# Multiply and GELU on one core: an early store of the first 4096 columns, between two loads on the same queue

## The chip, the cores and the metric

The kernel runs on one NeuronCore of a Trainium2 chip. The metric is the device time of one execution in microseconds; lower is better. Times are medians of several executions. The profile is of one execution, taken by the hardware profiler.

## What is computed

Two float32 arrays of 1024 x 4096 are multiplied element by element, and the product goes through the tanh form of GELU. The output has the same shape and type.

```python
def reference(x, y):          # both (1024, 4096) float32
    z = x * y
    return (0.5 * z * (1 + np.tanh(np.sqrt(2 / np.pi) * (z + 0.044715 * z ** 3)))).astype(np.float32)
```

Each array has 16.78 MB, so 33.55 MB are read and 16.78 MB are written.

## The kernel before

*Layout.* Each of the 128 partitions holds 8 rows of the array, which makes 32768 columns a partition. All of x stays in the on-chip buffer `xs` (128 x 32768), is multiplied there in place, goes through GELU in place, and is stored from there. The buffer `ys` holds half as much (16384 columns), so the second half of y overwrites the first.

*Stages.* The transfers are listed at the top of the file. x is loaded in two halves (x0 and x1, 8.39 MB each). y is loaded as a half (y0) and two quarters (y1 and y2, 4.19 MB each); y1 goes to the first half of `ys`, y2 to the second. The output is stored in two halves, store 0 and store 1. Compute works in steps of 4096 columns (`STEP`), eight in all: VectorE multiplies a step (line 87) once the loads it belongs to have landed, and counts `sem_mul` up by one; ScalarE then applies GELU to the step (line 94) and counts `sem_act` up by one. No step waits for a store.

*Order of the transfers.* There is no scheduler: all transfers are issued by SP, on one queue, in the order written in the code. x0 and y0 are hoisted ahead of the start-up barriers (`_hoist`). Behind these comes x1. Then each of y1 and y2 waits on `sem_mul`, since it overwrites what earlier multiplies read: y1 waits for two multiplies, y2 for four (line 77). Behind both loads SP waits for four activations and issues store 0, waits for eight and issues store 1 (lines 98 to 100), and last waits for the completion of both stores.

*What the steps touch.* `X_LOADS`, `Y_LOADS`, `STEP` and `STORES` (lines 13 to 17) define the pieces; `load_x` and `load_y` issue loads; each transfer has a semaphore of its own that reaches 16 when all of it has landed.

Of the kernel before, what the change touches and what calls it, by code (L numbers as in the profile page):

```python
# [1 line left out]

# [4 lines left out]


F32 = mybir.dt.float32
GELU = mybir.ActivationFunctionType.Gelu_apprx_tanh  # L10


X_LOADS = [(0, 16384), (16384, 32768)]

Y_LOADS = [(0, 16384, 0), (16384, 24576, 0), (24576, 32768, 8192)]
STEP = 4096
STORES = [(0, 16384), (16384, 32768)]
Y_RING = 16384


def _hoist(nc, issued):

    here = nc.cur_bb.bb.instructions
    first = nc.main_func.blocks[0].instructions
    for ins in issued:
        del here[next(k for k, i in enumerate(here) if i is ins or i.name == ins.name)]
    engine = issued[0].engine
    at = next(
        k
        for k, i in enumerate(first)  # L30
        if i.engine == engine and type(i).__name__ == "InstDrain"
    )
    first[at:at] = issued


@with_exitstack
def kernel(
    ctx: ExitStack,
    tc: tile.TileContext,
    x: bass.AP,  # L40
    y: bass.AP,
    out: bass.AP,
):
    nc = tc.nc
    P = nc.NUM_PARTITIONS

    x_r = x.flatten_outer_dims().rearrange("(p a) c -> p (a c)", p=P)
    y_r = y.flatten_outer_dims().rearrange("(p a) c -> p (a c)", p=P)
    out_r = out.flatten_outer_dims().rearrange("(p a) c -> p (a c)", p=P)
    total_f = x_r.shape[1]  # L50


    tc.close()
    tc.compile()  # L54

    xs = nc.alloc_sbuf_tensor("xs", [P, total_f], F32).ap()
    ys = nc.alloc_sbuf_tensor("ys", [P, Y_RING], F32).ap()
    sem_x = [nc.alloc_semaphore(f"sem_x{i}") for i in range(len(X_LOADS))]
    sem_y = [nc.alloc_semaphore(f"sem_y{i}") for i in range(len(Y_LOADS))]
    sem_o = [nc.alloc_semaphore(f"sem_o{i}") for i in range(len(STORES))]  # L60
    sem_mul = nc.alloc_semaphore("sem_mul")
    sem_act = nc.alloc_semaphore("sem_act")

    def load_x(i):
        a, b = X_LOADS[i]
        return nc.sync.dma_start(out=xs[:, a:b], in_=x_r[:, a:b]).then_inc(sem_x[i], 16)  # L66

    def load_y(i):
        a, b, r = Y_LOADS[i]
        return nc.sync.dma_start(  # L70
            out=ys[:, r : r + b - a], in_=y_r[:, a:b]
        ).then_inc(sem_y[i], 16)

    _hoist(nc, [load_x(0).ins, load_y(0).ins])
    load_x(1)
    for i in (1, 2):
        nc.sync.wait_ge(sem_mul, (Y_LOADS[i][1] - Y_LOADS[1][0]) // STEP)
        load_y(i)

    n = 0  # L80
    for i, (a, b, r) in enumerate(Y_LOADS):
        for j, (xa, xb) in enumerate(X_LOADS):
            if xa <= a < xb:
                nc.vector.wait_ge(sem_x[j], 16)
        nc.vector.wait_ge(sem_y[i], 16)  # L85
        for c in range(a, b, STEP):
            nc.vector.tensor_mul(  # L87
                out=xs[:, c : c + STEP],
                in0=xs[:, c : c + STEP],
                in1=ys[:, r + c - a : r + c - a + STEP],  # L90
            ).then_inc(sem_mul, 1)
            n += 1
            nc.scalar.wait_ge(sem_mul, n)
            nc.scalar.activation(  # L94
                out=xs[:, c : c + STEP], in_=xs[:, c : c + STEP], func=GELU
            ).then_inc(sem_act, 1)

    for i, (a, b) in enumerate(STORES):
        nc.sync.wait_ge(sem_act, b // STEP)
        nc.sync.dma_start(out=out_r[:, a:b], in_=xs[:, a:b]).then_inc(sem_o[i], 16)  # L100
    for i in range(len(STORES)):
        nc.sync.wait_ge(sem_o[i], 16)
    nums = sorted(s.num for s in [*sem_x, *sem_y, *sem_o, sem_mul, sem_act])
    assert nums == list(range(nums[0], nums[-1] + 1))
    nc.sync.sem_clear(range(nums[0], nums[-1] + 1))


# [1 line left out]
_INS = ['x', 'y']  # L109
_OUTS = [((1024, 4096), 'float32')]  # L110


# [23 lines left out]
```

## Time and profile before

| | us |
|---|---|
| median of 4 executions | 120.97 (120.87 to 121.22) |
| the profiled execution | 120.84 |
| its span, from the first instruction to the last | 119.5 |
| VectorE, mean of one multiply (x8) | 4.421 |
| ScalarE, mean of one activation (x8) | 3.617 |
| issue to landing: x0 and x1 | 21.9 and 58.7 |
| issue to landing: y0, y1, y2 | 40.8, 20.2, 22.0 |
| issue to landing: store 0 and store 1 | 37.7 and 26.1 |

The span lies within the profiled execution's time; what is outside it is start and end of the launch. Issue to landing runs from the issuing instruction on SP to the last of the 16 semaphore counts, so it holds the time that a transfer stood in the queue behind others. DMA share is the mean busy share of the 16 DMA engines of the core. In a cut of the span into stretches each packet counts where it begins, so a cut through a packet gives odd rates, and stretches are to be cut where the packets of a transfer begin.

### The profile page before, as it was taken

How to read it: one execution, taken by the hardware profiler on the slowest of the kernel's cores; microseconds unless marked ns; L12 is line 12 of the kernel's file. 1: busy time of each engine (PE TensorE's matmuls, PEld its weight loads, DVE VectorE, ACT ScalarE, POOL GpSimd, SP SyncE). 2: the span in 40 equal slices, each digit the busy share in tenths (PEclk: the TensorE clock that was granted, in tenths of full speed). 3: DMA queues.
4: the chain of work that ended last, by engine and by line, in shares of the span. 5: the costliest groups of instructions: out<-in, count | busy, mean ns of one | idle time of the engine just before them, and what ended most of it. 6: DMA issues, size and time to landing. Idle time of an engine off the chain costs nothing.

```text
span 119.5 us, 68 instructions
## 1 busy us (share of the span) xinstructions
DVE 35.0 (29%) x8; ACT 30.2 (25%) x9; POOL 0.2 (0%) x4
## 2 busy tenths in 40 slices
DVE  0000000000000199999600049949990000000000
ACT  3000000000000006797780000977479200000000
POOL 0000000000000000000000000000000000000000
DMA  9889888988899889988898989898899888988890
GB/s 351 351 351 702 351 351 351 680 373 351 351 570 483 351 351 504 548 351 351 373 504 351 526 351 515 362 526 351 351 504 548 351 351 373 680 351 351 351 680 22
DMA packets 1008, 50.33 MB, mean 421 GB/s; under 512 B 112, under 2 KB 112, under 8 KB 112
## 3 DMA queue, kind: packets, MB, share of 16 engines
q1 hardware_dynamic: 1008, 50.33, 98.5%
HBM read 33.55 MB, written 16.78 MB: 421 GB/s over the span
## 4 chain that ended last, share of the span: by engine, by line
DMA 53%; DVE 22%; ACT 3%; SPq 0%; issue 0%; DVEq 0%
DMA ys<-in_y_dram 53%; DVE xs L87 22%; ACT xs L94 3%; SPq L66 0%; DVEq L85 0%
## 5 line engine op out<-in xcount | busy, mean ns | idle before, releaser
L87 DVE TENSOR_TENSOR xs<-xs,ys 128x4096 f32<-128x4096 f32 x8 | 35.0, 4421 | 54.7 <-DMA ys<-in_y_dram 54.7
L94 ACT ACTIVATE xs<-xs 128x4096 f32<-128x4096 f32 x8 | 28.9, 3617 | 61.1 <-DVE xs L87 61.1
L94 ACT ACT_TABLE_LOAD x1 | 1.3, 1283 | 1.9 <-PEq L54 1.9
L120 POOL MEMSET const-bfloat16-1.0<- 128x1 bf16 x1 | 0.1, 101 | 0.0
L120 POOL MEMSET const-uint8-127<- 128x1 uint8 x1 | 0.1, 101 | 0.0
L120 POOL MEMSET const-float32-0.0<- 128x1 f32 x1 | 0.1, 98 | 0.2 <-issue 0.2
L120 POOL MEMSET const-float32-1.0<- 128x1 f32 x1 | 0.1, 98 | 0.0
## 6 DMA issues: line engine op xcount, KB each, us to landing
ys<-in_y_dram SPq DMA_DIRECT2D x2, 4096.0 KB, 21.1
xs<-in_x_dram SPq DMA_DIRECT2D x2, 40.3
out_dram<-xs SPq DMA_DIRECT2D x2, 31.9
ys<-in_y_dram SPq DMA_DIRECT2D x1, 40.8
```

The source lines that it names most:

```text
L87: nc.vector.tensor_mul(out=xs[:, c : c + STEP], in0=xs[:, c : c + STEP], in1=ys[:, r + c - a : r + c - a + STEP],).then_inc(sem_mul, 1)
L94: nc.scalar.activation(out=xs[:, c : c + STEP], in_=xs[:, c : c + STEP], func=GELU).then_inc(sem_act, 1)
L120: nc = _bacc.Bacc("TRN2", target_bir_lowering=False, num_devices=1)
```

## The change

The output is stored in three pieces instead of two: columns 0 to 4096, 4096 to 16384 and 16384 to 32768. The code that waits for the activations and issues a store becomes a function, `store(i)`. The first store is issued behind x1 and ahead of y1; the other two stay behind all loads. Loads and compute are as before.

```diff
-STORES = [(0, 16384), (16384, 32768)]
+STORES = [(0, 4096), (4096, 16384), (16384, 32768)]
...
+    def store(i):
+        a, b = STORES[i]
+        nc.sync.wait_ge(sem_act, b // STEP)
+        nc.sync.dma_start(out=out_r[:, a:b], in_=xs[:, a:b]).then_inc(sem_o[i], 16)
+
     _hoist(nc, [load_x(0).ins, load_y(0).ins])
     load_x(1)
+    store(0)
     for i in (1, 2):
         nc.sync.wait_ge(sem_mul, (Y_LOADS[i][1] - Y_LOADS[1][0]) // STEP)
         load_y(i)
...
-    for i, (a, b) in enumerate(STORES):
-        nc.sync.wait_ge(sem_act, b // STEP)
-        nc.sync.dma_start(out=out_r[:, a:b], in_=xs[:, a:b]).then_inc(sem_o[i], 16)
+    store(1)
+    store(2)
     for i in range(len(STORES)):
         nc.sync.wait_ge(sem_o[i], 16)
```

## The prediction

> **What bounds the kernel now.** I read the page first, then the chain of waits, the timeline with the landing times, and last the DMA share in stretches between the landings.
>
> The page says who is busy:
>
> ```profile
> DVE 35.0 (29%) x8; ACT 30.2 (25%) x9; POOL 0.2 (0%) x4
> DMA packets 1008, 50.33 MB, mean 421 GB/s; under 512 B 112, under 2 KB 112, under 8 KB 112
> q1 hardware_dynamic: 1008, 50.33, 98.5%
> ```
>
> The 16 DMA engines are occupied for 98.5% of the span and the compute engines for under a third. All bytes go over one queue, and the change moves the same 50.33 MB, so time can only come from how evenly that queue is fed and drained.
>
> The chain of waits names compute on the path (a share of 22% for VectorE), but that is the way the inference walks back: y loads wait for a multiply to free their buffer. The timeline shows that this wait is covered:
>
> ```profile
> 45.79 3.62 ACT L94 ACTIVATE xs<-xs 128x4096 f32<-128x4096 f32 x1 [42.58 <-DVE xs L87]
> 50.12 9.00 SPq L70 DMA_DIRECT2D ys<-in_y_dram  x2
> 62.44 31.20 SPq L100 DMA_DIRECT2D out_dram<-xs  x2
> 80.86 8.76 DVE L87 TENSOR_TENSOR xs<-xs,ys 128x4096 f32<-128x4096 f32 x2 [1.71 <-DMA ys<-in_y_dram]
> 89.66 3.62 ACT L94 ACTIVATE xs<-xs 128x4096 f32<-128x4096 f32 x1 [0.72 <-DVE xs L87]
> ```
>
> The reader should see that the second y load is issued at 50.12 and the first store at 62.44, each while earlier transfers still fill the queue. The groups by tile give issue-to-landing times, from which the landings follow: x0 at 21.9; y0 at 0.43 + 40.8 = 41.2; x1 at 1.93 + 58.7 = 60.6; y1 at 50.12 + 20.2 = 70.3; y2 at 58.79 + 22.0 = 80.8; store 0 at 62.44 + 37.7 = 100.1; store 1 at 93.30 + 26.1 = 119.4. The steps are 19.3, 19.4, 9.7, 10.5, 19.3, 19.3. One stands out: y2 carries the same 4.19 MB as y1 and takes 0.8 longer. It is the last load ahead of a store. Cut by where the packets of each transfer begin (x0, y0, x1, y1, y2, store 0, store 1; stretch, length, engines, clock, DMA share, GB/s):
>
> ```profile
> 1.00:21.00 20.00, 0.00 (x0) 1.28 (x1) 0.00 (x0) 1.00 1.01 419
> 21.00:40.30 19.30, 0.00 (x0) 0.00 (x0) 0.00 (x0) 1.00 1.00 435
> 40.30:59.70 19.40, 17.43 (x4) 11.75 (x4) 0.00 (x0) 1.00 1.00 432
> 59.70:69.40 9.70, 0.00 (x0) 2.72 (x1) 0.00 (x0) 1.00 1.00 432
> 69.40:79.80 10.40, 8.76 (x2) 4.23 (x2) 0.00 (x0) 1.00 1.00 403
> 79.80:99.10 19.30, 8.76 (x2) 10.24 (x3) 0.00 (x0) 1.00 1.00 435
> 99.10:118.40 19.30, 0.00 (x0) 0.00 (x0) 0.00 (x0) 1.00 1.00 435
> ```
>
> Loads and stores run at the same 432 to 435 GB/s. Only two stretches are below it: the first (20.0 instead of 19.3, the start of an empty queue) and y2's (10.4 instead of 9.7). In the second the share stays 1.00: no packet was missing, the last ones took longer. So the span is 1.0 before the first packet, 0.7 of start-up, 115.9 of bytes (5 x 19.3 for the large transfers, 2 x 9.7 for y1 and y2), 0.7 at the one turn from loading to storing, and 1.2 for the spread between the engines and the last completion.
>
> **What the Trainium skill says.** "DMA: Bandwidth & Descriptors", section Queues, rings and completion order: each DMA engine consumes its descriptors in ring order. The trace agrees: landings come in order of issue. So the new store will really stand between x1 and y1 and push y1 and y2 back. The section Two DMAs through the same engine are not ordered adds that descriptors are pipelined and an engine's read and write sides are separate queues; that fits the absence of any gap between y0 and x1 (435, then 432 GB/s)[...]. The section Latency and other measured facts gives about 0.6 us to a first byte for this kind of queue; here no packet begins before 1.0 us after the issue, and the trace's number is used.
>
> **The change part by part.** Numbering the stores anew: S0 (columns 0 to 4096, 2.10 MB), S1 (4096 to 16384, 6.29 MB), S2 (16384 to 32768, 8.39 MB).
>
> 1. *Instructions.* SP gets one more DMA and one more wait. The multiplies, the activations and every other DMA stay. On SP the new wait (first activation, done at 45.79 + 3.62 = 49.41) stands ahead of the y1 issue, which today goes at 50.12 when two multiplies are done. S0 costs SP about 0.35 (a store issue lasts 344 to 347 ns), so SP is free again at 49.8, before 50.12. No one waits longer. If it were later, the x1 load, which fills the queue until 59.7, would cover it by 9 us. Cost 0.
>
> 2. *Bytes.* S0 takes 2.10/435 = 4.8 us in the middle and the stores behind are shorter by the same 4.8. Net 0. The packets get smaller, 16 and 48 KB a row instead of 64 KB; from 64 to 32 KB the rate went from 435 (432 beside compute) to 432, so 0 to 0.1; I take 0.
>
> 3. *Turn from load to store.* It now happens twice, after x1 and after y2. The one seen cost 10.4 - 9.7 = 0.7. Add 0.7; bounds 0.5 to 0.8.
>
> 4. *Turn from store to load.* New, and not in the trace. Nearest row: the start of the queue, 20.0 - 19.3 = 0.7 for a first load whose reads have nothing in front of them. That is the upper bound (0.8 with rounding). The lower one is below nothing: if the 0.7 of step 3 only means that a store runs later in the pipeline than a load, the return gives it back (-0.7). I take +0.1: the y1 reads are queued 9 us before they are due, so an engine's read side can begin them while its write side still drains S0. If it then runs ahead of its writes by what the turn of step 3 cost (0.7), that hides all but 0.1 of a first read's latency. It is an estimate from those two stretches.
>
> 5. *The last loads come later, and the cover of the last store shrinks.* y2 lands 4.8 + 0.7 + 0.1 = 5.6 later, at 86.4. Two multiplies and an activation follow as today (80.8 to 93.28: 12.5), so S2 is issued near 98.9. Today that issue comes at 93.30 with the queue busy until 99.1 or so: 5.8 of cover. After, S1 occupies 14.5 instead of 19.3 (19.3 x 0.75), from about 85.4 to 99.9. Cover: 1.0. An issue needs 1.0 to 1.4 us until its packets begin (no packets before 1.0; all 16 engines begin between 1.0 and 1.4), so S2's packets are ready at 99.9 to 100.3. The cover is just gone: a gap of 0 to 0.4, and a store that starts unpipelined may pay up to the 0.7 of a cold start besides. But the 16 engines do not end S1 together (in the trace they begin store 1 spread over 99.1 to 99.8), and the engine that ends last sets the time; for it the descriptors arrive about in time. I take +0.15; bounds 0 and 0.9.
>
> Sum: 0 + 0 + 0.7 + 0.1 + 0.15 = +0.95 us. The profiled execution was 120.84 (span 119.5 and 1.3 around it); it would become 121.8. The median shown is 120.97, 0.13 above, so 121.9. Nothing is gained because the stored bytes do not overlap anything they did not already: the queue was full in the stretch where S0 is put, and it was full where S0 is taken from.
>
> **Rivals.**
> - *The return to loading costs a full start* (0.7 to 0.8 instead of 0.1). For it: the only cold first load seen costs that. Against: that one had an empty queue, this one has descriptors waiting. 121.9 + 0.65 = 122.6.
> - *The last store arrives late for all engines*, so that it starts cold: 0.9 instead of 0.15 in step 5. For it: 1.0 of cover against 1.0 to 1.4 needed. 121.9 + 0.75 = 122.7.
> - *The turns cancel*: the return gives back what the first turn took. For it: nothing in the trace excludes it, and store streams are as fast as load streams. Then only step 5 is left: 121.1.
> - *Faster: a store among loads overlaps them.* Mechanism: at both edges of S0 an engine reads in one direction while it writes in the other, and moves more than 435 GB/s. The price at most is all of S0 hidden, 4.8 us: 116.1; with a quarter of it hidden, about 119.8. It decides once the two edges hide more than the 0.95 above. Against: the one turn there is runs at 403, below either stream.
> - *The change doesn't do what it says*: S0 would have to leave SP after 59.7, but its activation ends at 49.41. I give this no share.
>
> **How the numbers follow.** Forecast 0.56, cold return 0.21, late last store 0.08, cancelling turns 0.10, overlap 0.05. About 0.2% (0.24 us) is what a measurement of this kernel can tell from no change. Cancelling turns at 121.1 is within it for the most part (0.09); overlap is faster (0.05); the rest is slower (0.86). The low end of the range, 121.2, is the forecast with 0.5 in step 3, 0 in step 4 and next to nothing in step 5; the high end, 123.0, has a cold return and half the bound of step 5. Outside lie the overlap, most of the cancelling turns and both rivals of the slow side together.
>
> **What would show it.** In the trace after: S0 issued near 49.4 and y1 still at 50.1 (step 1). The x1 stretch, up to the first S0 packet, at 20.1 instead of 19.4 (step 3). S0 landing near 66; y1 landing 9.7 to 9.8 later if step 4 is right, 10.4 if the return is cold, 9.0 if it gives back. y2 landing near 86.4, its stretch again 10.4. S2 issued near 98.9, and packets of S1 and S2 following each other with a gap of 0 to 0.4 (step 5). What would make it wrong: a y2 landing before 85.7 (the turns cancel or overlap), or a stretch below 435 GB/s in S0 itself, from the 16 KB packets.

## The result, and the profile after

The changed kernel takes 121.30 us (median of 37 executions, 121.06 to 121.98), the kernel before 120.97 (57 executions). The ratio is 1.0031, 95% interval 1.0024 to 1.0037: by this ratio it is slower by 0.37 us (the two medians alone differ by 0.33). The profiled execution took 121.21 us, its span is 119.9.

The page of the changed kernel, the lines that answer to those shown of before:

```profile
DVE 35.0 (29%) x8; ACT 30.2 (25%) x9; POOL 0.2 (0%) x4
DMA packets 1152, 50.33 MB, mean 420 GB/s; under 512 B 128, under 2 KB 128, under 8 KB 128
q1 hardware_dynamic: 1152, 50.33, 98.5%
```

There are 144 packets more: 128 of data (one packet is one row of a transfer, moved by one DMA engine) and 16 *completion writes* (packets of 4 bytes, one for each DMA engine, that count the transfer's semaphore up). The bytes and the share of 98.5% are the same. Nothing in these lines tells where 0.37 us went.

Its timeline (start, duration, engine, line, what; issues of one group are merged into one row):

```profile
45.70 3.62 ACT L100 ACTIVATE xs<-xs 128x4096 f32<-128x4096 f32 x1 [42.51 <-DVE xs L93]
49.34 0.35 SPq L77 DMA_DIRECT2D out_dram<-xs  x1
50.03 9.00 SPq L70 DMA_DIRECT2D ys<-in_y_dram  x2
62.35 36.44 SPq L77 DMA_DIRECT2D out_dram<-xs  x2
86.02 8.76 DVE L93 TENSOR_TENSOR xs<-xs,ys 128x4096 f32<-128x4096 f32 x2 [0.95 <-DMA ys<-in_y_dram]
94.81 3.62 ACT L100 ACTIVATE xs<-xs 128x4096 f32<-128x4096 f32 x1 [0.72 <-DVE xs L93]
```

The early store leaves SP at 49.34, and the y1 issue at 50.03 is not delayed by it. The last two multiplies start 5.2 us later than before (86.02 against 80.86), not 5.6. The last store is issued at 62.35 + 36.44 - 0.34 = 98.45.

Cut by where the packets of x1, S0, y1, y2, S1 and S2 begin (stretch, length, busy time of VectorE, ScalarE and GpSimd, granted clock, DMA share, GB/s):

```profile
40.30:60.60 20.30, 17.43 (x4) 12.74 (x4) 0.00 (x0) 1.00 1.00 413
60.60:65.50 4.90, 0.00 (x0) 1.73 (x1) 0.00 (x0) 1.00 0.99 425
65.50:75.20 9.70, 0.00 (x0) 0.00 (x0) 0.00 (x0) 1.00 1.01 434
75.20:84.90 9.70, 8.60 (x2) 3.62 (x1) 0.00 (x0) 1.00 1.01 432
84.90:99.40 14.50, 8.93 (x3) 10.85 (x3) 0.00 (x0) 1.00 1.00 434
99.40:118.70 19.30, 0.00 (x0) 0.00 (x0) 0.00 (x0) 1.00 1.00 435
```

A *turn* below is the change from a load to a store that follows it in the queue, a *return* the change back. x1's stretch grew from 19.4 to 20.3: the turn into S0 costs 0.9. But y2's shrank from 10.4 to 9.7: the turn into S1, in the same place where before paid 0.7, costs next to nothing. The price of the turn has moved, it has not doubled. y1 behind S0 takes 9.7, so the return to loading is free. S2 follows S1 with no stretch below 434.

Steps of a tenth of a microsecond are coarse for this, so from here on an *excess* is also given: from the trace's packet records, the mean over the 16 engines of the time between the completion writes of two successive transfers, less the time of the bytes (2.4145 us for a row of 64 KB on one engine, as in the undisturbed stretch of y0, in proportion for others, and 0.006 for the completion write). The table has both kernels, each with a second profile (below):

```
excess, us          x1     S0     y1     y2     first store behind the loads    last store
before             0.02    -     0.02   0.75    0.00                            0.00
before, again      0.02    -     0.02   0.68    0.00                            0.00
changed            0.97   0.03   0.02   0.07    0.01                            0.03
changed, again     0.95   0.03   0.03   0.12    0.01                            0.00
```

The sums are 0.79 and 0.72 before, 1.13 and 1.14 after: 0.34 to 0.42 more, and the measured 0.37 lies between. The packets show where the price sits: of the eight packets that each engine moves for x1, the last takes 3.35 us in the mean in the changed kernel and the one before it 2.43; in the kernel before both take about 2.42. So it is the end of the load that is late, not the store. (The expectations below were written with an earlier reading of the same packets, which gives a little less: 0.73 and 0.93 for 0.75 and 0.97.)

### The profile page after: what moved, and what is told of

The parts are those of the page before. It is cut to its first block, busy times and chain, and to the rows that moved or that the text cites. A ratio compares the mean times of both kernels' runs of the same rounds, so it can differ in the third digit from the quotient of the medians.

```text
span 119.9 us, 69 instructions
## 1 busy us (share of the span) xinstructions
DVE 35.0 (29%) x8; ACT 30.2 (25%) x9; POOL 0.2 (0%) x4
## 3 DMA queue, kind: packets, MB, share of 16 engines
q1 hardware_dynamic: 1152, 50.33, 98.5%
## 4 chain that ended last, share of the span: by engine, by line
DMA 57%; DVE 22%; ACT 3%; SPq 0%; issue 0%; DVEq 0%
DMA ys<-in_y_dram 57%; DVE xs L93 22%; ACT xs L100 3%; SPq L66 0%; DVEq L91 0%
```

## Experiments

SBUF below is the on-chip memory that holds `xs` and `ys`; HBM holds x, y and the output. Three questions: is the price of a turn paid once or at each turn; what is it; and why does the change still cost 0.37, when one payment replaces another?

All times beside the kernel before on the same chip (medians, ratio with 95% interval where timed):

| kernel | us | ratio to before |
|---|---|---|
| split alone, nothing moved | 120.93 | 1.0005 [0.9996, 1.0013] |
| two early stores of 2048 | 121.25 | 1.0026 [1.0016, 1.0036] |
| early store of 128 columns | 120.88 | 1.0000 [0.9991, 1.0008] |
| early store of 512 | 120.61 | 0.9973 [0.9963, 0.9982] |
| early stores of 512, twice | 120.66 | 0.9978 [0.9969, 0.9986] |
| early store of 1024 | 120.93 | 1.0001 [0.9991, 1.0011] |
| early store of 2048 | 121.14 | 1.0019 [1.0012, 1.0026] |
| early store of 4096, one load later | 121.22 | 1.0035 [1.0020, 1.0050] |
| early store of 8192 | 125.46 | 1.0376 [1.0358, 1.0394] |
| changed, last store cut in two | 121.36 | 1.0038 [1.0024, 1.0051] |
| changed, x1 as two quarters | 121.23 | 1.0029 [1.0020, 1.0038] |
| before with an HBM to HBM copy | 123.24 | 1.0189 [1.0169, 1.0209] |
| before with an SBUF to SBUF copy | 123.70 | 1.0223 [1.0201, 1.0244] |

### The split without the move

```diff
     load_x(1)
-    store(0)
...
+    store(0)
     store(1)
     store(2)
```

> The output in three stores (4096, 12288 and 16384 columns), all behind the loads: the split without the move. Theory F (the first store of an execution pays once, 0.7 to 0.9 us, wherever it stands; later turns from load to store are free): y2's stretch is 10.4 to 10.6 us as in the kernel before, nothing else is longer, the time is that of before within 0.15 us. Theory R (the price hangs on the packets of the store that follows: 64 KB 0.7, 16 KB 0.9, 48 KB 0.04): y2's stretch is 10.6 and the time is 0.2 us above before.

The time is that of before, so cutting the stores costs nothing by itself and the 0.37 belongs to the move. In the profiled execution the stretches of y2 and S0 are

```profile
69.40:79.80 10.40, 8.76 (x2) 4.17 (x2) 0.00 (x0) 1.00 1.02 403
79.80:84.70 4.90, 3.66 (x1) 3.07 (x1) 0.00 (x0) 1.00 0.99 425
```

with an excess of 0.91 at y2. This execution took 121.06, 0.13 above the median of its kind, so its turn may have been dearer than usual. A second profile:

> The split alone once more. If small packets of the first store make the turn dear: y2's stretch is again longer by 0.85 to 1.0 us. If 0.90 was the spread of one execution: 0.6 to 0.8.

gave 0.81 (one straggling engine made that execution 121.52). So the small rows of the store may add a little to a turn (0.91 and 0.81 against 0.75 and 0.68), but not enough to be seen in 13 timed executions.

### Once or at each turn

```diff
-STORES = [(0, 4096), (4096, 16384), (16384, 32768)]
+STORES = [(0, 2048), (2048, 4096), (4096, 16384), (16384, 32768)]
...
         load_y(i)
+        if i == 1:
+            store(1)
...
-    store(1)
     store(2)
+    store(3)
```

> The early 4096 columns as two stores of 2048, one after x1 and one after y1, so there are three turns from load to store. Theory F: x1's stretch is longer by 0.9 us, those of y1 and y2 by under 0.1, and the time is that of the changed kernel, 0.3 to 0.5 us above before. Theory R (every turn into a store of small packets with loads behind it costs about 0.9): x1's and y1's stretches are both longer by 0.9 and the time is 1.2 to 1.4 us above before.

x1, early store, y1, early store, y2, later store:

```profile
40.10:60.50 20.40, 17.43 (x4) 12.52 (x4) 0.00 (x0) 1.00 0.99 411
60.50:63.00 2.50, 0.00 (x0) 1.94 (x1) 0.00 (x0) 1.00 0.96 406
63.00:72.60 9.60, 0.00 (x0) 0.00 (x0) 0.00 (x0) 1.00 1.02 440
72.60:75.10 2.50, 1.45 (x1) 0.00 (x0) 0.00 (x0) 1.00 0.96 406
75.10:84.80 9.70, 7.32 (x2) 5.97 (x2) 0.00 (x0) 1.00 1.01 436
84.80:99.30 14.50, 8.76 (x2) 8.50 (x3) 0.00 (x0) 1.00 1.00 434
```

(The engines are up to 0.6 us apart and each packet counts where it begins, so short stretches come out a little under or over 435.) Three turns, and only the first costs: the excess is 0.91 at x1, 0.02 at y1, 0.02 at y2. A price at each turn is ruled out. With the early store one load later the price goes with it (y1 has rows of 32 KB, x1 rows of 64 KB):

> The changed kernel with the early store of 4096 columns moved on by one load, to between y1 and y2. Theory F: x1's stretch is 19.4, y1's is longer by 0.7 to 0.9 us, y2's is 9.7; the time is 0.2 to 0.5 us above before. If only the place right after x1 is dear: y1's stretch is longer by under 0.3, and y2's may be longer again.

x1, y1, the early store and y2:

```profile
40.30:59.60 19.30, 17.43 (x4) 11.50 (x4) 0.00 (x0) 1.00 1.00 435
59.60:70.20 10.60, 0.00 (x0) 2.97 (x1) 0.00 (x0) 1.00 1.00 396
70.20:75.00 4.80, 3.46 (x1) 0.00 (x0) 0.00 (x0) 1.00 1.01 434
75.00:84.80 9.80, 5.30 (x2) 7.23 (x2) 0.00 (x0) 1.00 1.02 430
```

There the excess is 0.03 at x1, 0.95 at y1, and 0.26 at y2; the time is 0.42 above before. The profiled execution was the slowest of its kind (121.73 against a median of 121.22), so the 0.26, more than the forecast allows, may belong to that one execution.

### How the price depends on the bytes of the first store

The early store was cut to 128, 512, 1024 and 2048 columns, for example

```diff
-STORES = [(0, 4096), (4096, 16384), (16384, 32768)]
+STORES = [(0, 512), (512, 16384), (16384, 32768)]
...
-        nc.sync.wait_ge(sem_act, b // STEP)
+        nc.sync.wait_ge(sem_act, -(-b // STEP))
```

> Only 128 columns (0.07 MB) are stored after x1, all others behind the loads. Theory F: x1's stretch is still longer by 0.7 to 0.9 us and y2's is 9.7; the time is 0 to 0.4 us above before. If the price goes with the bytes or the packets of the early store (R): x1's stretch is longer by under 0.3, and y2's is 10.4 again, since a store of 64 KB packets follows it; the time is within 0.2 us of before.

> 512 columns early (2 KB rows, 0.26 MB, 0.6 us of bytes), the rest behind the loads. Theory L (the price of a turn is a lead that an engine's reads of SBUF take over its writes; it is built up once, is at most about 0.9 us of bytes, can't be larger than the store that builds it, and is kept over later loads): x1's stretch is longer by 0.4 to 0.65 us and y2's by the remainder, 0.1 to 0.4. Theory F (the first store pays all, whatever its size; against it already 128 columns, which paid about 0.1 and left 0.5 for y2): x1's stretch longer by 0.1 only, or by 0.9 with nothing left for y2. Time for both 0 to 0.2 above before, since the last store is issued long before it is due.

> 1024 columns early (4 KB rows, 1.2 us of bytes). Theory L with the sizes measured so far: x1's stretch longer by 0.5 to 0.8 us, y2's by 0.05 to 0.15, and the time between that of 512 columns (0.3 below before) and that of 2048 (0.2 above): -0.2 to +0.1. If the gain of 512 columns was chance: within 0.1 of before here as well.

> 2048 columns early, which leaves about 3.4 us of cover for the last store instead of 1.0. Theory C: the time is that of before within 0.15 us. Theory T: x1's turn and the small packets cost the same as in the changed kernel, so 0.25 to 0.45 above before. Both: x1's stretch longer by 0.85 to 0.95 and y2's by under 0.1.

```
columns    bytes of it at 435 GB/s    excess x1    S0     y2     time against before
   128          0.15 us                 0.10      0.09   0.54     0.0
   512          0.60                    0.30      0.04   0.29    -0.3
  1024          1.2                     0.83      0.04   0.02     0.0
  2048          2.4                     0.99      0.03   0.02    +0.2
  4096          4.8                     0.97      0.03   0.07    +0.4
```

The 512 columns show the division best; x1, S0, y1, y2 and the large store:

```profile
40.20:59.90 19.70, 17.43 (x4) 11.96 (x4) 0.00 (x0) 1.00 1.00 426
59.90:60.60 0.70, 0.00 (x0) 0.70 (x1) 0.00 (x0) 1.00 0.67 258
60.60:70.30 9.70, 0.00 (x0) 1.80 (x1) 0.00 (x0) 1.00 1.02 441
70.30:80.20 9.90, 8.76 (x2) 3.71 (x2) 0.00 (x0) 1.00 1.01 424
80.20:98.90 18.70, 8.76 (x2) 10.75 (x3) 0.00 (x0) 1.00 1.00 435
```

The stretches take 19.7 and 9.9 instead of 19.4 and 10.4: a part is paid at each turn. No payment at x1 is above the bytes of the store behind it, and what is left at y2 falls as x1's grows. That the first store pays all whatever its size is ruled out. These sizes fit a price that a store builds up with its bytes, to an upper limit, and that then stays paid. The forecasts of x1's share were too high for 512 columns (0.4 to 0.65, measured 0.30) and a little too low for 1024 (0.5 to 0.8, measured 0.83). With 128 columns neither theory had the 0.54 at y2: one forecast nothing there, the other the full 0.7. That the time fell below before with 512 was not expected. The time with 2048, 0.22 above before, lies between the ranges of its two theories.

### Reads of SBUF or writes to HBM

Two copies of 2048 columns in the place of the early store, in the kernel before: one that writes HBM without reading SBUF, one that reads SBUF without writing HBM. Each has a semaphore of its own, `sem_c`; ahead of the first store SP waits for the copy to HBM, ahead of the y2 load for the copy in SBUF.

```diff
+    sem_c = nc.alloc_semaphore("sem_c")
...
+    nc.sync.wait_ge(sem_act, 1)
+    nc.sync.dma_start(out=out_r[:, 0:2048], in_=x_r[:, 0:2048]).then_inc(sem_c, 16)
...
+    nc.sync.wait_ge(sem_c, 16)
```

```diff
+    sem_c = nc.alloc_semaphore("sem_c")
...
+    nc.sync.wait_ge(sem_act, 1)
+    nc.sync.wait_ge(sem_mul, 3)
+    nc.sync.dma_start(out=ys[:, 8192:10240], in_=xs[:, 0:2048]).then_inc(sem_c, 16)
...
+        if i == 2:
+            nc.sync.wait_ge(sem_c, 16)
         load_y(i)
```

> The kernel before with a copy of 2048 columns of x from HBM to HBM after x1, into the output, where the first store later overwrites it: a write to HBM whose reads are like a load's. Its 1.05 MB are 2.4 us of bytes more. Theory L (reads of SBUF run ahead of the writes): x1's stretch is longer by under 0.2, nothing of the lead is built, and y2's turn still costs 0.6 to 0.9. Theory W (the first writes to HBM of an engine are what costs): x1's stretch is longer by 0.8 to 1.0 and y2's by under 0.1.

> The kernel before with a copy of 2048 columns from SBUF to SBUF after x1, into a part of ys that y2 overwrites later: reads of SBUF without any write to HBM, 2.4 us of bytes more. Theory L: x1's stretch is longer by 0.8 to 1.0 and y2's by under 0.1, as with a store. Theory W: x1's stretch as before, and y2's turn still costs 0.6 to 0.9.

HBM to HBM: x1, the copy, y1 and y2:

```profile
40.30:59.70 19.40, 17.43 (x4) 11.78 (x4) 0.00 (x0) 1.00 1.00 432
59.70:62.10 2.40, 0.00 (x0) 2.40 (x1) 0.00 (x0) 1.00 0.98 410
62.10:71.80 9.70, 0.00 (x0) 0.29 (x1) 0.00 (x0) 1.00 1.02 439
71.80:82.10 10.30, 8.76 (x2) 4.06 (x2) 0.00 (x0) 1.00 1.01 407
```

SBUF to SBUF, the same four:

```profile
40.20:60.80 20.60, 17.43 (x4) 12.94 (x4) 0.00 (x0) 1.00 1.00 407
60.80:63.20 2.40, 0.00 (x0) 1.52 (x1) 0.00 (x0) 1.00 0.97 410
63.20:72.90 9.70, 0.00 (x0) 0.00 (x0) 0.00 (x0) 1.00 1.02 439
72.90:82.60 9.70, 8.61 (x2) 3.62 (x1) 0.00 (x0) 1.00 1.00 432
```

The HBM copy leaves x1 at 19.4 and y2 pays in full (excess 0.73). The SBUF copy makes x1 pay 1.21 (more than the 0.8 to 1.0 forecast), and y2 nothing (0.02), although no byte has yet been written to HBM. So the price comes with the first reads from SBUF behind loads; writes to HBM neither bring it nor are needed for it. In both kernels the same store of 64 KB rows follows y2, so the rows of that store don't decide whether the turn there costs something. Each of the two rests on one profile.

### The cover of the last store

```diff
-STORES = [(0, 4096), (4096, 16384), (16384, 32768)]
+STORES = [(0, 4096), (4096, 16384), (16384, 24576), (24576, 32768)]
...
     store(2)
+    store(3)
```

> The changed kernel with its last store cut in two (16384 to 24576 and 24576 to 32768), so that the first half is issued after six activations, some 10 us earlier, and the second has 10 us of cover. Theory C (the 0.37 us that the change costs are the cover of the last store, gone in most executions): the time falls by 0.25 to 0.4 us, to that of before within 0.15. Theory T (they are the dearer turn after x1, 0.9 instead of 0.7 us, and the smaller packets): the time stays 0.25 to 0.45 above before.

*Cover* is the time for which the queue is still busy when the last store is issued. The time does not fall: the ratio is 1.0038 where the changed kernel has 1.0031. The last store's cover is not where the 0.37 went. (The excess in this execution: 1.09 at x1, 0.07 at y2.) That the cover can be lost, with twice the early columns:

> 8192 columns early instead of 4096. Theory C: the second store then covers 9.7 us instead of 14.5, and y2 lands 4.9 later; the last store's packets begin 4.4 to 4.9 us after the second store has ended, and the time is 4.4 to 5.1 above the changed kernel's, 125.7 to 126.4. Theory T alone, with cover enough: 121.3 to 121.5.

The end of S1 and S2, and the issue of S2 from the timeline of the same kernel:

```profile
89.70:99.40 9.70, 8.74 (x3) 7.23 (x2) 0.00 (x0) 1.00 1.00 432
99.40:104.10 4.70, 0.21 (x1) 3.62 (x1) 0.00 (x0) 1.00 0.00 0
104.10:123.50 19.40, 0.00 (x0) 0.00 (x0) 0.00 (x0) 1.00 1.00 432
```

```profile
103.29 0.34 SPq L77 DMA_DIRECT2D out_dram<-xs  x1
```

Each DMA engine stands still for 4.5 us in the mean: S2 is issued at 103.29, when the engines have been done with S1 for 3.2 to 3.9 us, and its packets begin 0.8 to 1.0 later. The time, 125.46, is 4.2 above the changed kernel's and 4.5 above before; the forecast (4.4 to 5.1 above the changed kernel's) was a little high. At 4096 columns the cover is just enough: there the issue at 98.45 is followed by S2's packets from 99.47 on, on engines that end S1 at 99.43 to 100.02.

### Why the change still costs 0.37

> The changed kernel once more. If the dear turn is steady: x1's stretch is longer by 0.9 to 1.05 us again, y2's by 0 to 0.1. If it is the spread: 0.65 to 0.85.

It took 121.15, with 0.95 at x1 and 0.12 at y2: the dearer turn is steady. Two ways to account for it were tried. The first is loads queued behind the store (the y1 and y2 loads are taken out):

```diff
-    for i in (1, 2):
-        nc.sync.wait_ge(sem_mul, (Y_LOADS[i][1] - Y_LOADS[1][0]) // STEP)
-        load_y(i)
...
-        nc.vector.wait_ge(sem_y[i], 16)
+        if i == 0:
+            nc.vector.wait_ge(sem_y[i], 16)
```

> The changed kernel without the y1 and y2 loads: the second half is multiplied with y0's data again, so the second half of y is left out of the computation. S0 still follows x1, with no load behind it. If loads queued behind a store make its turn dear: x1's stretch is longer by 0.65 to 0.8 us. If it is the place after x1 or the packets of 16 KB: 0.88 to 1.05.

x1 and S0 there:

```profile
40.30:60.80 20.50, 17.43 (x4) 12.68 (x4) 0.00 (x0) 1.00 1.00 409
60.80:65.60 4.80, 3.76 (x1) 1.79 (x1) 0.00 (x0) 1.00 1.00 430
```

The whole takes 105.11, since 8.39 MB of loads are missing. With no load behind it the turn costs 1.12, more than either range, so loads behind do not make it dear. The second is the rows of the load ahead (x1 has 64 KB, y2 has 32 KB):

```diff
-X_LOADS = [(0, 16384), (16384, 32768)]
+X_LOADS = [(0, 16384), (16384, 24576), (24576, 32768)]
...
     load_x(1)
+    load_x(2)
     store(0)
```

> The changed kernel with x1 loaded as two quarters, so that the load ahead of the early store has rows of 32 KB instead of 64. Theory Q (the packets of the load ahead set the price: 64 KB 0.95, 32 KB 0.75): the stretch of the second quarter is 9.7 + 0.65 to 0.85 us, and the time is 0.1 to 0.3 below the changed kernel's, 121.0 to 121.2. Theory X (the place): 9.7 + 0.9 to 1.1, and the time is the changed kernel's, 121.2 to 121.4.

The second quarter of x1, S0, y1 and y2:

```profile
50.00:60.40 10.40, 8.81 (x3) 8.79 (x3) 0.00 (x0) 1.00 1.00 403
60.40:65.20 4.80, 0.00 (x0) 2.06 (x1) 0.00 (x0) 1.00 1.00 430
65.20:74.90 9.70, 0.00 (x0) 0.00 (x0) 0.00 (x0) 1.00 1.01 436
74.90:84.80 9.90, 8.62 (x2) 3.62 (x1) 0.00 (x0) 1.00 1.00 424
```

In this profile the turn after x1 falls to 0.78, as theory Q said, but y2 now pays 0.17, and the time (121.23) is hardly below the changed kernel's. With the store one load later (above) the load ahead had rows of 32 KB too, and the turn cost 0.95, so these rows are not shown to set the price. The reverse, 64 KB rows ahead of the turn in the kernel before:

> The kernel before with the second half of y as one load (rows of 64 KB), issued after four multiplies. Its turn to the first store comes at about 79 to 80 us. Theory Q: this load's stretch is 19.35 + 0.9 to 1.1 us. Theory X: 19.35 + 0.65 to 0.8. The whole is slower for another reason: four multiplies come after the last load, 8.8 us later than two would end, so the last store's issue comes 2 to 4 us after the first store has ended, 123 to 125.5.

settled nothing: its time was 127.03, above the range expected. Its last load was issued at 58.75, too late to follow x1 without a gap, and one engine ended that load 1.7 us after the mean of the others, so the excess of 2.4 at that load mixes a cold start, the turn and the laggard.

## Why the prediction was right or wrong

The direction was right; the size was wrong, +0.37 against +0.95. That 121.30 lies inside the stated range is luck. The low end, 121.2, is said to be the forecast with 0.5 in step 3 and next to nothing in steps 4 and 5, but 120.97 + 0.5 is 121.5, and by its own working the range would have begun there, above the measured time.

*Step 1* (S0 and the y1 issue) held: 49.34 and 50.03. *Step 2* held: the smaller rows cost 0.03 for S0 and 0.01 for S1.

*Step 3 is the step that failed*: "It now happens twice, after x1 and after y2. The one seen cost 10.4 - 9.7 = 0.7. Add 0.7". It happens twice but is paid, all but a small rest, once. The term was right as an amount for a first turn, wrong as an addition. What stood in its place: 0.97 instead of 0.02 at x1, and 0.07 instead of 0.75 at y2, so +0.27 (+0.37 by the second profiles: 0.95 instead of 0.02, and 0.12 instead of 0.68). The reading that the runs support: behind the last load packets an engine begins to read SBUF for the store; while it does, the load's last bytes come later, and from then on the reads are ahead of the writes by that much. This lead is kept over later loads, so a second turn finds it already there. Shown are that the load's last packets are late (3.35 us instead of 2.42), that it takes reads of SBUF, that the price grows with the bytes of the first store up to 0.9 to 1.2 us, and that after the one or two loads that follow the next turn costs little (0.02 to 0.26). That the engine's reads run ahead of its writes is inferred, and no run looks inside the engine. The prediction had the idea in hand in step 4, where a read side that "runs ahead of its writes" was to hide the return's latency, and did not ask what becomes of this lead at the next turn.

*Step 4* (return to loading, +0.1) was right within its error: y1 has an excess of 0.02 with S0 ahead of it, and the same 0.02 with x1 ahead of it. The rival of a cold return is refuted by y1 (9.7), that of cancelling turns by the same number, since the return gives nothing back (y1 would have taken 9.0). The overlap did not occur: no stretch of the changed kernel runs above 435.

*Step 5* (+0.15) was close: the cover is just used up, but the join of S1 and S2 costs only 0.03 and 0.00 in the two profiles. Restoring the cover gains nothing; doubling the early columns loses another 4.2, so the arithmetic of cover holds to within some tenths.

By these terms the sum is 0.27 + 0.03 + 0.01 + 0.03 = +0.34 (by the second profiles 0.37 + 0.03 + 0.01 + 0.00 = +0.41). What stays open is why the change does not come out at zero. All turns together cost 0.95 to 1.21 in every profile with an early store of 1 MB or more and loads behind it (1.04 and 1.07 for the changed kernel, 0.95 with x1 in quarters, 1.21 with the store one load later), while the one turn of the kernel before costs 0.68 and 0.75. The split alone, whose one turn leads into rows of 16 KB, lies between, with 0.91 and 0.81. Loads behind the store are excluded as the reason by the one profile without them (1.12). Smaller rows in the load ahead went with a cheaper first turn in one kernel (0.78) and not in another (0.95). Why a single turn at the end of the loads gets by with less is not known.

## What to carry to other kernels

Cut a trace by its transfers, look for the stretches whose rate is below the stream's, and before adding such a cost once more, run a kernel in which the event happens twice: a price seen once doesn't tell whether it is paid each time or only the first time. When stores are moved forward, count how long the store in front of the last one still covers the last step of compute: 4096 early columns used that up here, and 8192 made the kernel 4.5 us slower than before. A very short early store, 512 columns, beat the kernel before by 0.3 us and the changed one by more, which is a measured effect of this kernel and no rule.

## What the runs showed that was not expected

- Copies from HBM to HBM and from SBUF to SBUF run in the middle of the loads at the rate of a load (2.4 us for 1.05 MB), and differ in the turn: an excess at x1 of 0.04 against 1.21 us.
- Dividing the lead between two turns was cheaper than paying it at one: with 512 columns 0.30 + 0.29 against 0.75 at once, and 0.3 us less in time. The excess accounts for about half of that gain; where the rest comes from was not tried. With 128 columns (0.10 at x1, 0.09 at S0, 0.54 at y2) and with 1024 (0.83 at x1) there was no gain. A second store of 512 columns, behind y1, added nothing:

> 512 columns early after x1 and 512 after y1. One such store took 0.24 at x1 and left 0.28 at y2, and the kernel was 0.3 us faster than before. Theory L: the second finds most of the lead built, so y1's stretch is longer by 0.05 to 0.25 and y2's by 0 to 0.15; the time is 0.2 to 0.5 us below before. Theory R (each early store pays on its own): y1's stretch longer by 0.25 again, y2's by 0.28 or more, and the time no better than before by more than 0.1.

The time was in theory L's range, but y1 had an excess of 0.02, less than that theory's 0.05 to 0.25, and y2 also 0.02: nothing was left for them. The profiled execution of this kernel was its slowest (121.31 against a median of 120.66), and its 1.10 at x1 is not to be read as the turn alone: 0.43 is in x1's last packet, and 0.69 in the seven before it, which have at most 0.12 in every other profile in which x1 is one load. Why 0.43 sufficed here, when one store of 512 columns left 0.29 for y2, is open.

- One execution differs from another by about 0.1 us in the turn alone (0.81 and 0.91 for the split). For the kernel before:

> The kernel before, once more, for a second profile of its turn from y2 to the first store: 0.7 as in the first profile if the price is steady, up to 0.9 if the difference between 0.73 there and 0.93 after x1 in the changed kernel is only that of one execution from another.

It took 120.81, and its turn cost 0.68 instead of 0.75.
